# Six weight tiles loaded during the attention: the low parts by ScalarE negation and an accumulating DMA, in place of GpSimd and VectorE subtractions

## The chip, the cores and the metric

The kernel runs on one core of one Trainium2 chip. The metric is the device time of one execution in microseconds, the lower the better. The kernel before took 905.79 us in the median of three runs (904.6 to 907.33).

A core has five engines with instruction queues of their own: PE (TensorE, matrix products), DVE (VectorE), ACT (ScalarE), POOL (GpSimd) and SP (SyncE, which here only issues DMAs). Each works its queue strictly in order, so an instruction that waits holds up all that stand behind it on its engine.

## The reference

One layer of an encoder block over 512 tokens and 16 meta tokens, with 1024 channels. Cut to its main lines:

```python
h = rms_norm(h_res, norm_mix_g[i])
proj = h @ w_in[i]
u, q, k, v, g_ssm, g_attn = jnp.split(proj, split_at, axis=-1)
y_ssm  = ...                 # two-directional state space model on u, GELU, gate
y_attn = gqa_attention(...)  # 16 query heads, 4 key/value heads, softmax over 528 keys
merged = (sigmoid(g_ssm) * (y_ssm @ w_ssm_proj[i])
          + sigmoid(g_attn) * (y_attn @ w_attn_proj[i]))
h_res = h_res + merged @ w_out[i]
h2 = rms_norm(h_res, norm_mlp_g[i])
h_res = h_res + square(relu(h2 @ w_mlp_in[i])) @ w_mlp_out[i]
```

All of it is in float32.

## The kernel before

**Split products.** To get float32 accuracy from the faster matmul type, every operand is split into a high part (a cast to fp32r) and a low part (the operand less its high part). `mm3` issues three matmuls for one product: high by high, high by low and low by high (L159 to L161).

**Loading a weight tile.** `load_w` (L107) makes three tiles of 128 x 1024 values: `wf` by a DMA of 512 KB from SP (L112), `wh` by casts on ACT (L98), and `wl` in one of two ways. The one is a subtraction `wf - wh` on POOL or DVE (L125). The other writes `-wf`, cast to fp32r, into `wl` on ACT (L122) and then lets a DMA issued from POOL add `wf` onto it (L123); what is left in `wl` is the rest that the cast cut off. Which way is taken is `W_ENG[0](i)`: the engine for the low part, or None for the DMA. Each of the three tags has two buffers, so the tiles of load i take the place of those of load i-2, and nothing of a load can be written before the matmuls that read load i-2 are done.

**The attention.** The loop over 16 heads and 4 steps per head issues, for each step: scores of the next head (`sc`, L1102), the maximum on DVE (`mx`, L1106), the exponential on ACT (L1111), the reciprocal of the sum on DVE (`rsm`, L1115), the product on POOL (`ea` or `zT`, L1116), transposes on PE (`atr`, L1126), the split of the transposed block into `ph` on ACT (L98) and `pl` on DVE (L103), and with a lag the matmuls with V (`pv`, L1176). `pvout` copies the result with two ACT copies (`ybuf`, L1146 and L1148).

**Filler.** Between these steps `pump` feeds PE with other work, in the order of `fill_q`: the projections of query groups 2 and 3 (`t_qfull`: two tiles each, matmuls `adp<-wh,hTh` and the like) and five tiles of the attention gate (`t_gate`: one tile each, 24 matmuls `adp<-hTh,wh` and the like). After a query projection its norm and rotation (`norm_rope`) run in small pieces on ACT, DVE and POOL. The casts and low parts of these tiles go through the queue `bgq`, from which `bg_pop` takes three at a time; a scheduler then sets the final order on each engine from priorities and its own model of times.

Nine tiles are loaded for this filler. The first three (query group 2 and the first gate tile) are split with the setting of the stage ahead. The other six, called A to F below, are split with the line

```python
W_ENG[0] = lambda i: (S, WA(V, S, Q)[i % len(WA(V, S, Q))])   # L1166, WA gives (Q, V)
```

so their low parts are made in turn on POOL (A, C, E) and DVE (B, D, F), in two halves of 128 x 512 each. A and B are the two tiles of query group 3, C to F are gate tiles. The same setting serves the tiles after the attention (`w_attn`, `w_out`).

Of the kernel before, what the change touches and what calls it, by code (L numbers as in the profile page):

```python
# [14 lines left out]
ALU = mybir.AluOpType  # L15
# [29 lines left out]
WA = lambda V, S, Q: (Q, V)  # L45
# [25 lines left out]
def hybrid_block(ctx, tc, x, meta, w_in, w_glu, w_ssm, w_attn, w_out, w_m1, w_m2,  # L71
# [3 lines left out]
    V, S, Q, PE = nc.vector, nc.scalar, nc.gpsimd, nc.tensor  # L75
# [16 lines left out]
    W_ENG = [lambda i: (S, Q if i % 2 else V)]  # L92
# [3 lines left out]
    def copy_on(eng, o, i):  # L96
        if eng is S:
            return S.copy(out=o, in_=i)  # L98
        return eng.tensor_copy(out=o, in_=i)
# [8 lines left out]
    def load_w(src, kt, cols):  # L108
        wf = wp.tile([128, kt, cols], F32, tag="wf", bufs=2, name="wf")
        wh = wp.tile([128, kt, cols], F32R, tag="wh", bufs=2, name="wh")  # L110
        wl = wp.tile([128, kt, cols], F32R, tag="wl", bufs=2, name="wl")
        nc.sync.dma_start(out=wf, in_=src.rearrange("(k p) c -> p k c", p=128))  # L112
        i = wcount[0]
        wcount[0] += 1
        eh, el = W_ENG[0](i)
        nh, nl = WS_H[0], 1 if el is None else WS_Q[0] if el is Q else WS_H[0]

        def part(j, n, lo):
            r = slice(kt * j // n, kt * (j + 1) // n)
            if lo and el is None:  # L120

                S.activation(out=wl[:, r], in_=wf[:, r], func=AF.Copy, scale=-1.0)  # L122
                Q.dma_start(out=wl[:, r], in_=wf[:, r], accum_op=ALU.add)  # L123
            elif lo:
                el.tensor_tensor(out=wl[:, r], in0=wf[:, r], in1=wh[:, r].bitcast(F32), op=ALU.subtract)  # L125
            else:
                copy_on(eh, wh[:, r], wf[:, r])
        ops = [(j, nh, False) for j in range(nh)] + [(j, nl, True) for j in range(nl)]
        if bg_on[0]:
            ops = [(j, nh, False) for j in range(nh)] + [(0, 1, True)] if el is None else \  # L130
                [(j, nh, lo) for j in range(nh) for lo in (False, True)]
        for o in ops:
            if bg_on[0]:
                bgq.append((i, lambda o=o: part(*o)))
            else:
                part(*o)
        return wh, wl
# [207 lines left out]
    def t_u(c, res):  # L345
        def run(w):
            wh, wl = w
            H = L // 2
            uT = su1.tile([128, L], F32, tag="uT", bufs=2, name="uT")
            res[c] = uT  # L350
            for hf in range(2):
                ps = dps("ups")[:, :H]
                sl = slice(hf * H, hf * H + H)
                for k in range(KD):
                    mm3(ps, wh[:, k, :], wl[:, k, :], hTh[:, k, sl], hTl[:, k, sl], k == 0, k == KD - 1)
                    yield 0.33
                S.copy(out=uT[:, sl], in_=ps)
        return Task(lambda: load_w(w_in[:, c * 128:c * 128 + 128], KD, 128), run, cost=2 * KD * 0.33)

    def t_gate(m, base, dst, alloc):  # L360
        def run(w):
            ps = alloc()
            for k in range(KD):
                mm3(ps, w[0][:, k, :], w[1][:, k, :], hRh[:, k, :], hRl[:, k, :], k == 0, k == KD - 1)
                yield 0.65
            S.copy(out=dst[:, m, :], in_=ps)
        return Task(lambda: load_w(w_in[:, base + m * 128:base + m * 128 + 128], KD, 128), run, cost=KD * 0.65)

    def load256(base):
        return [load_w(w_in[512 * j:512 * j + 512, base:base + 256], 4, 256) for j in range(2)]  # L370
# [792 lines left out]
    bg_on[0] = True  # L1163
    brk[0] = True
    LBc[0] = LBA
    W_ENG[0] = lambda i: (S, WA(V, S, Q)[i % len(WA(V, S, Q))])  # L1166
    lag = []

    def pv_next():
# [46 lines left out]
    h_st.close()  # L1216


    WS_H[0], WS_Q[0] = 1, 1
    h2_st = ExitStack()  # L1220
    h2p = h2_st.enter_context(tc.tile_pool(name="h2p", bufs=1, side="right", reuse_waits="tile"))
# [34 lines left out]
    for m in range(KD):  # L1256
        wh, wl = load_w(w_attn[:, m * 128:m * 128 + 128], KD, 128)
# [323 lines left out]
```

## Time and profile before

| | before |
|---|---|
| median of three runs | 905.79 us |
| profiled execution, its time | 902.95 us |
| profiled execution, its span | 901.0 us |
| PE busy | 844.8 us, 94% |
| DVE busy | 676.2 us, 75% |
| ACT busy | 521.9 us, 58% |
| POOL busy | 193.2 us, 21% |

The span runs from the first to the last instruction on the chip; 1.95 us lie around it. PE is the busiest engine over the whole. The attention loop runs from about 282 to 467 us. Busy shares over the span say little of one stage, so the attention is read from windows, from waits and from the instructions in order of time.

### The profile page before, as it was taken

What the parts mean: (1) busy time and instruction counts of PE and PEld (TensorE: products, weight loads), DVE (VectorE), ACT (ScalarE), POOL (GpSimd) and SP (SyncE); (2) the same over time, 40 slices, a digit from 0 to 9 for tenths busy, and PEclk for the clock granted to TensorE, in tenths of its full rate; (3) what the DMA queues carried; (4) which work ended last, traced back from release to release, by engine and by line L of the source; (5) the groups of instructions that cost most, each with busy time, mean ns of one, the idle gap of its engine ahead of it and who ended that gap; (6) DMA issues with size and microseconds to landing.
All of it is one profiled execution on the core that took longest, in us unless ns stands there. A gap on an engine that the chain in (4) does not pass through costs nothing.

```text
span 901.0 us, 13081 instructions
## 1 busy us (share of the span) xinstructions
PE 844.8 (94%) x4798; PEld 721.6 (80%) x4798; DVE 676.2 (75%) x1217; ACT 521.9 (58%) x916; POOL 193.2 (21%) x185
## 2 busy tenths in 40 slices
PE   6989999978998989799989999999999999999994
PEld 4988888767886979688878888888888888888884
DVE  6997799779898697867775536747767577776687
ACT  5446776547745557578784245656555655555543
POOL 1001100001021567566534450010100010000000
PEclk9999999999999999999999999999999999999998
DMA  7245533212122020011024343466656556575302
GB/s 240 68 98 113 130 83 78 76 48 70 56 87 71 29 70 5 21 46 49 20 77 134 111 142 119 149 163 164 161 143 164 147 157 168 136 187 134 100 1 93
DMA packets 97473, 92.52 MB, mean 103 GB/s; under 512 B 4465, under 2 KB 79793, under 8 KB 97410
## 3 DMA queue, kind: packets, MB, share of 16 engines
q1 hardware_dynamic: 87824, 69.25, 25.3%
q0 software_dynamic: 5168, 18.40, 10.6%
q10 hardware_dynamic: 4418, 4.04, 1.6%
q8 instruction: 38, 0.62, 0.3%
q14 instruction: 25, 0.20, 0.1%
HBM read 69.03 MB, written 2.10 MB: 79 GB/s over the span
## 4 chain that ended last, share of the span: by engine, by line
PE 74%; DVE 14%; ACT 6%; DMA 3%; issue 3%; POOL 1%; DVEq 0%; ACTq 0%; POOLq 0%; SPq 0%
PE m L161 6%; PE m L160 6%; PE m L159 6%; PE o L161 5%; PE o L159 5%; PE o L160 5%; PE pv L1176 3%; PE sc L1102 2%; PE atr L1126 2%; DVE wl L125 2%; PE gps L159 2%; PE gps L161 2%; PE gps L160 2%; PE adp L159 2%; PE adp L160 2%
## 5 line engine op out<-in xcount | busy, mean ns | idle before, releaser
L98 ACT CAST wh<-wf 128x512 fp32r<-128x512 f32 (+1 forms) x120 | 90.0, 778 | 99.8 <-PE m L160 60.7
L1447 DVE TENSOR_TENSOR ybuf<-o,ybuf 128x1024 f32<-128x1024 f32 x52 | 63.6, 1222 | 67.9 <-PE o L161 67.8
L123 POOL DMA_DIRECT2D wl<-wf x35 | 30.3, 865 | 377.4 <-ACT wl L122 299.5
L161 PE MATMUL m<-h2h,wl 128*128 128x512 f32 (+1 forms) x272 | 102.4, 377 | 0.8 <-DVE wl L125 0.8
L160 PE MATMUL m<-h2l,wh 128*128 128x512 f32 (+1 forms) x272 | 102.5, 377 | 0.2 <-DVE h2l L103 0.2
L159 PE MATMUL m<-h2h,wh 128*128 128x512 f32 (+1 forms) x272 | 102.3, 377 | 0.3 <-ACT h2h L98 0.2
L160 PE MATMUL o<-ol,fh 128*128 128x512 f32 (+1 forms) x216 | 83.2, 385 | 0.0
L159 PE MATMUL o<-oh,fh 128*128 128x512 f32 (+1 forms) x216 | 83.2, 385 | 0.0
L161 PE MATMUL o<-oh,fl 128*128 128x512 f32 (+1 forms) x216 | 83.2, 385 | 0.0
L125 DVE TENSOR_TENSOR wl<-wf,wh 128x512 fp32r<-128x512 f32 (+1 forms) x65 | 57.3, 900 | 13.4 <-ACT wh L98 13.2
L161 PEld LDWEIGHTS m<-h2h,wl 128*128 128x128 f32 x272 | 51.2, 188 | 10.5 <-DVE wl L125 1.3
L159 PEld LDWEIGHTS m<-h2h,wh 128*128 128x128 f32 x272 | 51.1, 188 | 10.1 <-ACT h2h L98 0.5
L160 PEld LDWEIGHTS m<-h2l,wh 128*128 128x128 f32 x272 | 51.2, 188 | 9.8 <-DVE h2l L103 0.4
L1106 DVE TENSOR_REDUCE mx<-sc 128x1 f32<-128x528 f32 x64 | 44.8, 702 | 12.7 <-PE sc L1102 11.9
L103 DVE TENSOR_TENSOR pl<-atr,ph 128x512 fp32r<-128x512 f32 x64 | 43.5, 684 | 9.3 <-ACT ph L98 8.5
L98 ACT CAST ph<-atr 128x512 fp32r<-128x512 f32 x64 | 37.1, 584 | 18.1 <-PE atr L1126 17.6
L161 PEld LDWEIGHTS o<-oh,fl 128*128 128x128 f32 x216 | 40.6, 188 | 8.1
L160 PEld LDWEIGHTS o<-ol,fh 128*128 128x128 f32 x216 | 40.6, 188 | 8.1
L159 PEld LDWEIGHTS o<-oh,fh 128*128 128x128 f32 x216 | 40.6, 188 | 8.0
L1116 POOL TENSOR_TENSOR ea<-zT,rsm 128x528 f32<-128x528 f32 x32 | 34.2, 1069 | 21.2 <-DVE rsm L1115 20.3
L122 ACT ACTIVATE wl<-wf 128x1024 fp32r<-128x1024 f32 x35 | 36.8, 1050 | 0.9 <-PE kvps L160 0.9
L1176 PE MATMUL pv<-ph,Vhl 128*128 128x256 f32 x128 | 34.6, 294 | 2.2 <-ACT ybuf L1148 1.4
(403 smaller groups left out, 2477.9 us busy)
## 6 DMA issues: line engine op xcount, KB each, us to landing
wl<-wf POOLq DMA_DIRECT2D x35, 512.0 KB, 4.4
wf<-in_w_in_dram SPq DMA_DIRECT2D x32, 512.0 KB, 4.0
wf<-in_w_m_dram SPq DMA_DIRECT2D x32, 512.0 KB, 4.1
q<-in_w_m_dram SPq DMA_DIRECT2D x32, 512.0 KB, 4.5
ybuf<-in_x_dram SPq DMA_DIRECT2D x8, 512.0 KB, 4.0
wf<-in_w_attn_dram SPq DMA_DIRECT2D x8, 512.0 KB, 4.0
wf<-in_w_out_dram SPq DMA_DIRECT2D x8, 512.0 KB, 3.2
wf<-in_w_ssm_dram SPq DMA_DIRECT2D x4, 512.0 KB, 3.5
```

The source lines that it names most:

```text
L98: return S.copy(out=o, in_=i)
L103: b = el.tensor_tensor(out=l, in0=src, in1=h.bitcast(F32), op=ALU.subtract)
L122: S.activation(out=wl[:, r], in_=wf[:, r], func=AF.Copy, scale=-1.0)
L123: Q.dma_start(out=wl[:, r], in_=wf[:, r], accum_op=ALU.add)
L125: el.tensor_tensor(out=wl[:, r], in0=wf[:, r], in1=wh[:, r].bitcast(F32), op=ALU.subtract)
L159: PE.matmul(out=o, lhsT=lh, rhs=rh, start=first, stop=False, skip_group_check=goes_on)
L160: PE.matmul(out=o, lhsT=lh, rhs=rl, start=False, stop=False, skip_group_check=goes_on)
L161: return PE.matmul(out=o, lhsT=ll, rhs=rh, start=False, stop=last, skip_group_check=goes_on)
L1106: g0 = V.tensor_reduce(out=mx, in_=sc[:, :, :NL], axis=AX.XY, op=ALU.max, negate=True)
L1116: pend.append(lambda: Q.tensor_tensor(out=en, in0=e, in1=rs_.to_broadcast([128, L]), op=ALU.mult))
L1176: PE.matmul(out=pvt[0][:, 256 * f:256 * f + 256], lhsT=vw, rhs=pw, start=left == [8, 9], stop=left == [0, 0])
L1447: V.tensor_tensor(out=x2q[r][h], in0=z, in1=x2q[r][h], op=ALU.add)
```

## The change

In the attention `W_ENG` gives None for the low part, so tiles A to F are made by ACT's negated copies and an accumulating DMA from POOL. The copies are made in two halves, the DMA once for the whole tile, and in the queue both casts now come ahead of both negations. Behind the attention the setting of before is put back, so `w_attn` and `w_out` are split as they were.

```diff
                 S.activation(out=wl[:, r], in_=wf[:, r], func=AF.Copy, scale=-1.0)
-                Q.dma_start(out=wl[:, r], in_=wf[:, r], accum_op=ALU.add)
+                if j == n - 1:
+                    Q.dma_start(out=wl, in_=wf, accum_op=ALU.add)
...
         if bg_on[0]:
-            ops = [(j, nh, False) for j in range(nh)] + [(0, 1, True)] if el is None else \
+            ops = [(j, nh, lo) for lo in (False, True) for j in range(nh)] if el is None else \
                 [(j, nh, lo) for j in range(nh) for lo in (False, True)]
...
-    W_ENG[0] = lambda i: (S, WA(V, S, Q)[i % len(WA(V, S, Q))])
+    W_ENG[0] = lambda i: (S, None)
...
     h_st.close()
+    W_ENG[0] = lambda i: (S, WA(V, S, Q)[i % len(WA(V, S, Q))])
     WS_H[0], WS_Q[0] = 1, 1
```

The new lines move the numbers: L123 becomes L124, lines below it go up by one, and those behind L1219 by two. Six DVE and six POOL subtractions leave, twelve ACT negations and six DMAs come in. SP's order is the same.

The scheduler also moves other instructions. On PE, around tile E (`adp<-hTh,wh` and its fellows are the gate matmuls, `sc`, `atr` and `pv` belong to the attention), before:

```order
L159 MATMUL adp<-hTh,wh 128x512
L160 MATMUL adp<-hTl,wh 128x512
L1102 MATMUL sc<-Kh,qst 128x264 x2
L1102 MATMUL sc<-Kl,qst 128x264 x2
L161 MATMUL adp<-hTh,wl 128x512
L159 MATMUL adp<-hTh,wh 128x512
L160 MATMUL adp<-hTl,wh 128x512
```

And in the changed kernel, 11 rows behind the same two matmuls with `wh`:

```order
L1177 MATMUL pv<-pl,Vhl 128x256
L1103 MATMUL sc<-Kh,qst 128x264 x2
L1103 MATMUL sc<-Kl,qst 128x264 x2
L1127 MATMUL atr<-ident,zT 128x128
L1127 MATMUL atr<-ident,ea_3210 128x128
L1127 MATMUL atr<-ident,zT 128x128
L1127 MATMUL atr<-ident,ea_3210 128x128
L162 MATMUL adp<-hTh,wl 128x512
L160 MATMUL adp<-hTh,wh 128x512
L161 MATMUL adp<-hTl,wh 128x512
```

The first gate matmul that reads E's `wl` now stands behind 20 attention matmuls more, and all 22 that are left of the tile stand there in one run. Before, 17 of the 22 were spread among those 20, and the last five stood at the same place.

On ACT, around the split of tile E (`gbuf` is the copy of tile D's result, `qst` a split of the queries), before:

```order
L1111 ACTIVATE zT,sm<-sc,mx 128x528
L98 CAST wh<-wf 128x512 x2
L990 CAST qst<-atr 64x512
L1111 ACTIVATE rt,sm<-sc,mx 128x528
L98 CAST ph<-atr 128x512
L990 CAST qst<-atr 64x512
```

And in the changed kernel:

```order
L1112 ACTIVATE zT,sm<-sc,mx 128x528
L98 CAST wh<-wf 128x512
L122 ACTIVATE wl<-wf 128x512
L98 CAST wh<-wf 128x512
L367 COPY gbuf<-adp 128x512
L991 CAST qst<-atr 64x512
L1112 ACTIVATE rt,sm<-sc,mx 128x528
L122 ACTIVATE wl<-wf 128x512
L98 CAST ph<-atr 128x512
```

One negation has moved in ahead of the exponential, the other behind it, ahead of the `ph` cast.

On POOL at the same place, before:

```order
L1116 TENSOR_TENSOR ea_3210<-zT,rsm 128x528
L125 TENSOR_TENSOR wl<-wf,wh 128x512 x2
L1116 TENSOR_TENSOR ea_3210<-rt,rsm 128x528
L1149 TENSOR_TENSOR ybuf<-ybuf 64x512
L125 TENSOR_TENSOR wl<-wf,wh 128x1024
```

And in the changed kernel:

```order
L1117 TENSOR_TENSOR ea_3210<-rt,rsm 128x528
L124 DMA wl<-wf 128x1024
L1117 TENSOR_TENSOR ea_3210<-zT,rsm 128x528
L1150 TENSOR_TENSOR ybuf<-ybuf 64x512
L124 DMA wl<-wf 128x1024
L126 TENSOR_TENSOR wl<-wf,wh 128x1024
```

E's DMA stands behind the product that stood behind E's subtractions, and F's DMA has come in ahead of the subtraction of the first `w_attn` tile.

Elsewhere in the attention, the gate matmuls of tile D (10 of 24) and most of the first pass of query group 3 move back by some 15 to 23 rows on PE; those of tiles C and F keep their places. On ACT both negations of B stand ahead of a `ph` cast, and those of C ahead of its own casts and of an exponential.

## Rows read from the trace of the kernel before

**Rows 1.** The page: span; busy us, share and instructions of PE.

```profile
span 901.0 us, 13081 instructions
PE 844.8 (94%) x4798; PEld 721.6 (80%) x4798; DVE 676.2 (75%) x1217; ACT 521.9 (58%) x916; POOL 193.2 (21%) x185
```

**Rows 2.** Windows: length, busy of PE, PEld, DVE, ACT, POOL; granted clock; DMA.

```profile
350.00:370.00 20.00, 16.27 (x124) 15.13 (x124) 16.19 (x35) 11.47 (x25) 13.21 (x12) 0.97 0.09 28
390.00:410.00 20.00, 20.00 (x133) 17.45 (x132) 14.27 (x28) 17.48 (x37) 14.06 (x13) 1.00 0.14 38
410.00:430.00 20.00, 17.85 (x135) 15.54 (x134) 15.33 (x30) 16.10 (x37) 15.24 (x13) 1.00 0.15 43
```

**Rows 3.** PE's waits, 275 to 465 us: us in total, times, longest.

```profile
PE atr L1126 <- DVE pl L103: 4.9, 6, 2.6
PE pv L1176 <- DVE pm L1140: 3.2, 4, 1.1
```

**Rows 4.** Low parts before, groups of 265:462 (busy, mean ns), then by time.

```profile
L125 POOL TENSOR_TENSOR wl<-wf,wh 128x512 fp32r<-128x512 f32 x6 | 7.6, 1294 | 0.0
...
331.84 2.61 DVE L125 TENSOR_TENSOR wl<-wf,wh 128x512 fp32r<-128x512 f32 x2
380.21 1.42 DVE L125 TENSOR_TENSOR wl<-wf,wh 128x512 fp32r<-128x512 f32 x1 [0.35 <-ACT wh L98]
```

**Rows 5.** ACT half tile, group of 265:462; L123: ns min/median/max; its landing.

```profile
L98 ACT CAST wh<-wf 128x512 fp32r<-128x512 f32 x22 | 12.6, 618 | 0.8 <-PE adp L161 0.7
...
L123 POOL DMA_DIRECT2D wl<-wf x35: 852/862/918, 55.8 to 842.9; - x35
...
DMA to landing us min/median/max: 4.4/4.4/6.2
```

**Rows 6.** By time, near tile A: start us, us; the wait in brackets.

```profile
319.94 1.22 DVE L171 TENSOR_SCALAR rst<-st 128x16 int32<-128x16 int32 x1
325.13 0.18 DVE L177 TENSOR_TENSOR rst<-rsy 128x16 f32<-128x16 f32 x1
327.07 0.52 PE L1102 MATMUL sc<-Kh,qst 128*128 128x264 f32 x2 [1.47 <-ACT zT L1111]
```

**Rows 7.** By time, near tile B.

```profile
330.92 0.59 ACT L98 CAST ph<-atr 128x512 fp32r<-128x512 f32 x1
331.57 0.38 PE L1176 MATMUL pv<-ph,Vhl 128*128 128x256 f32 x1 [0.68 <-ACT ph L98]
```

**Rows 8.** By time, near tile C.

```profile
355.17 1.14 ACT L98 CAST wh<-wf 128x512 fp32r<-128x512 f32 x2 [0.74 <-PE adp L161]
356.22 0.70 ACT L1111 ACTIVATE rt<-sc,mx 128x528 f32<-128x528 f32 x1
367.16 0.33 PE L1126 MATMUL atr<-ident,zT 128*128 128x128 f32 x1 [2.62 <-DVE pl L103]
```

**Rows 9.** By time, near tile D.

```profile
383.11 0.39 PE L1176 MATMUL pv<-ph,Vhl 128*128 128x256 f32 x1 [0.92 <-ACT ybuf L1148]
```

**Rows 10.** By time, tile E and what follows its last matmul.

```profile
399.87 0.70 ACT L1111 ACTIVATE rt<-sc,mx 128x528 f32<-128x528 f32 x1
402.30 1.08 POOL L1116 TENSOR_TENSOR ea<-rt,rsm 128x528 f32<-128x528 f32 x1
401.41 0.40 PE L161 MATMUL adp<-hTh,wl 128*128 128x512 f32 x1
401.64 0.40 PE L159 MATMUL adp<-hTh,wh 128*128 128x512 f32 x1
408.56 0.40 PE L161 MATMUL adp<-hTh,wl 128*128 128x512 f32 x1
408.76 1.05 ACT L98 CAST wh<-wf 128x1024 fp32r<-128x1024 f32 x1 [0.37 <-PE adp L160]
```

**Rows 11.** Windows over two idle stretches of PE and what followed; columns as above.

```profile
291.70:294.00 2.30, 0.00 (x0) 0.00 (x0) 2.30 (x3) 0.88 (x3) 2.30 (x3) 0.97 0.00 0
294.00:297.50 3.50, 3.49 (x17) 3.50 (x18) 1.41 (x4) 1.91 (x4) 2.63 (x3) 0.53 0.29 76
```

## The prediction

> **What bounds the kernel now.** I read the page's head first: 901.0 us of span, PE busy for 844.8 of them [rows 1]. The profiled execution took 902.95 us, so 1.95 us lie around the span; the median of the runs shown is 905.79 us, 2.84 us above it. Sums are made on the 902.95 and then moved by 2.84.
>
> Only the attention is edited, so next come windows of it. PE is busy for 16.27 of 20 us in one window, for all 20 in another and for 17.85 in a third [rows 2]. So PE sets the pace over long stretches and is stopped in short ones. PE's waits say by whom: most for DVE, 4.9 us for `pl` and 3.2 us for `pm` [rows 3]. An edit here pays only where it shortens one of these stops, and costs wherever it makes a new one, because PE works in order. Last I read the instructions in order of time around each of the six tiles, and compare when `wl` is ready with when PE asks for it.
>
> **The change, priced by kind.** Out go six POOL halves of 1.29 us, 7.6 us [rows 4], and six DVE halves; the two of B took 2.61 us together, one of D 1.42 us [rows 4], and 0.7 us each for the remaining three makes some 6 us. In come twelve ACT negations. The trace has no negation of a half tile, but a cast of the same shape takes 0.62 us [rows 5], or 0.57 in a row of two [rows 8], so 12 x 0.6 = 7 us on ACT. In come six DMA issues of 0.86 us on POOL, 5 us, and what matters more, each lands 4.4 us after its issue at the median, 6.2 at most [rows 5]. A subtraction of 1.3 us made `wl` ready; now the last negation, POOL's turn and 4.4 us stand in that place.
>
> The Trainium skill, page "DMA: Bandwidth & Descriptors", section "Anatomy of one DMA — SWDGE (gpsimd) path", gives about 2.0 us fixed and 436 KB per us, which for 512 KB is an estimate of 3.2 us. The 35 DMAs of this very kind in the trace say 4.4 [rows 5], and the measurement decides; by the page the forecast below would be 1.2 us lower.
>
> **The change, tile by tile.**
>
> A: POOL's two subtractions leave just where the small DVE steps of the query norm run. There such a step took 1.22 us, and 0.18 us a little later [rows 6]. Four of them were so long, and PE waited 1.47 us for the exponential behind them [rows 6]. POOL's rotation products move up and lengthen some of them again. I take one step's worth, -1.2 us; ends 0 and -2.5 (two steps and a half). A's `wl` is first read behind B's casts, which come after the gate tile between them is done, so its DMA costs nothing.
>
> B: both negations stand ahead of a `ph` cast for which PE already waited 0.68 us [rows 7]. They delay it by 1.14 us; some of it may be won back by DVE's 2.61 us. +0.9 us. PE's matmuls with B's `wl` were moved back, and by 4.4 us of landing they are met within about a microsecond; ends +0.3 and +2.2.
>
> C: the negations stand ahead of the casts at 355.17 and so push the exponential at 356.22 by 1.14 us [rows 8]. From there ACT's queue runs without a pause to the norm's square, DVE's small steps and the `pl` for which PE waited 2.62 us at 367.16 [rows 8]. +1.1 us; ends 0 (if DVE, not ACT, sets that stop) and +1.6 (if the DMA lands after PE's call too).
>
> D: one negation comes ahead of the `ph` cast and of the two `ybuf` copies, for the second of which PE waited 0.92 us [rows 9]. +0.6 us; ends 0 and +1.2. The matmuls were moved back by enough for the DMA.
>
> E is the largest. One negation pushes the exponential of 399.87 to about 400.4, the second follows it and ends near 401.9. The DMA stands behind POOL's product of 1.08 us [rows 10], which may now start at about 402.0. So issue is near 403.1 and landing near 407.5. PE ran E's `wl` matmuls from 401.41 to 408.56, 0.23 us apart [rows 10]. With 22 of them now in one run behind the attention's matmuls, PE can be there at 408.56 - 21 x 0.23 = 403.7, or, as an estimate, near 405 if two more negations of 0.57 us on ACT hold up the exponentials. It stands until 407.5 and starts the last of the 22 at 407.5 + 21 x 0.23 = 412.3, against 408.56: +3.7 us. Behind it on ACT stands the cast of the next `w_attn` tile, which waits for E's last matmul already now, 0.37 us [rows 10]; all `ph` casts queue behind that cast, so the attention itself is late by as much. Ends: 0, if the DMA lands by 404, and +5.4, with the clock (below).
>
> F: its matmuls come after a long stretch of attention work that hides the landing; 0, ends -0.6 and +0.6, a half negation either way. The source tiles are held until the DMA has landed instead of until the subtraction, so the loads behind them start later; a whole tile's matmuls lie between such a load and its use and hide that. If that cover were gone it would be 4.4 us a tile.
>
> Given back: behind E PE idles for 2.15 us between 410 and 430 [rows 2]. Part of that is waiting for DVE, which now catches up: -1.5 us; ends 0 and -2.2.
>
> Sum: -1.2 + 0.9 + 1.1 + 0.6 + 3.7 + 0 - 1.5 = **+3.6 us**, so 906.6 us for an execution like the profiled one and 905.79 + 3.6 = 909.4 us at the median. All low ends together are -5.0, all high ends +11.
>
> **The rivals.**
>
> *Faster, by relief of DVE and POOL.* PE waits on DVE for 4.9 + 3.2 us [rows 3], and small DVE steps are seven times longer beside POOL work [rows 6]. If `wl` lands before PE calls and the freed 6 us of DVE and 7.6 us of POOL come off the stops, half of those 8.1 us goes: 905.79 - 4.0 = 901.8. It decides at E: landing by about 404. Against it: the DVE steps that PE waits for mostly lie in A and C, and in C POOL's subtractions were over before them. The Trainium skill, page "GPSIMD Engine Reference", section "8. Key points", says that GpSimd and VectorE share SBUF interfaces and contend; by that rule DVE should gain, and the trace agrees for A.
>
> *Hidden.* From 390 to 410 PE is busy all the time [rows 2]; if PE has work in its queue for each delay and A's gain pays for B and C, the time is 905.8 within 2.7.
>
> *Slower still, by the clock.* After 2.30 us with no PE work the granted clock was 0.53 for 3.5 us [rows 11], half of full speed, the lower of the two levels; 3.5 x 0.47 = 1.6 us were lost. A stop of 2.5 us at E would do this again, and one at C makes a stop longer that is 2.62 us already: 909.4 + 1.6 to 909.4 + 3.3, so 911 to 912.7.
>
> That the change doesn't do what it says is left out: the order shows all six DMAs in place.
>
> **How the numbers follow.** The forecast, 909.4, has 0.38 (its own range 906.5 to 911); the clock on top of it 0.14; hidden 0.27; relief 0.21. A measurement of this kernel can tell about 0.3%, 2.7 us, from no change. Relief mostly falls beyond that, 0.18 of it, hidden wholly within, and of the forecast 0.03 falls within too. So faster 0.18, same 0.27 + 0.03 + 0.03 = 0.33, slower 0.35 + 0.14 = 0.49. To leave out no more than 2 in 10, the range goes from 902 (within relief) to 914.
>
> **What would show it.** Right: PE waiting for DMA `wl` at a gate matmul for 2 us or more near 405 us, the last matmul of E about 4 us later against the start of the attention, and ACT's first `w_attn` cast late by the same. The stop near 367 us longer by about 1 us. DVE's small steps near 320 us shorter. SP's waits no worse. Wrong: no wait of PE for `wl` at all, or an attention that ends earlier than before; then the landing or PE's arrival at E is mis-sized, or DVE was the bound all along.

## The result, and the profile after

The changed kernel took 914.68 us in the median of four executions (912.27 to 915.41), beside 905.19 us for the kernel before: a ratio of 1.0098, 95% interval 1.0082 to 1.0114. So it is slower, by 9.5 us where 3.6 were forecast, and the time lies just outside the range of 902 to 914. A second set of six executions, with a median of 914.55 us beside 905.55, gave the same ratio, 1.0098 (1.0067 to 1.0130).

The profiled execution took 912.27 us, 910.1 of them the span. The page's head, to be held against [rows 1]:

```profile
span 910.1 us, 13094 instructions
...
PE 850.9 (93%) x4798; PEld 725.2 (80%) x4798; DVE 669.2 (74%) x1211; ACT 528.4 (58%) x928; POOL 189.3 (21%) x185
```

ACT has 6.5 us more, DVE 7.0 and POOL 3.9 us less, much as priced. PE does the same 4798 matmuls and is busy 6.1 us longer: a busy PE that does no more work is a slower PE. Part of this is the pair of executions: the mean granted clock was 0.985 here and 0.991 in the profile before, where the kernel before has 0.987 on average. All of the difference arises in the attention or ahead of it. Both kernels compute 64 exponentials in the loop, in the same sequence, so each can be paired with its like. The one at the loop's start is 1.4 us later than before, although the instructions up to there are the same; that is spread between executions, not an effect of the change. The one behind tile E (423.82, before 414.72) is 9.1 us later, and so are all that follow, to the end. So 7.7 us of this pair arise in the attention.

Windows of the attention (length, busy of PE, PEld, DVE, ACT, POOL; granted clock; DMA):

```profile
330.00:350.00 20.00, 17.45 (x125) 16.25 (x126) 11.92 (x25) 13.62 (x32) 10.53 (x11) 0.91 0.33 80
360.00:390.00 30.00, 24.21 (x145) 20.41 (x142) 20.75 (x43) 18.64 (x40) 16.60 (x16) 0.89 0.15 36
390.00:410.00 20.00, 19.07 (x124) 16.05 (x123) 13.56 (x27) 15.71 (x36) 11.34 (x11) 1.00 0.25 57
410.00:430.00 20.00, 16.60 (x109) 14.04 (x108) 10.32 (x21) 13.84 (x29) 11.31 (x10) 1.00 0.52 129
```

The granted clock, 0.91 and 0.89 in the first two, was 1.00 and 0.94 over the same times before:

```profile
330.00:350.00 20.00, 17.47 (x139) 16.37 (x138) 16.42 (x29) 13.62 (x31) 11.90 (x11) 1.00 0.09 27
360.00:390.00 30.00, 25.14 (x154) 21.69 (x153) 24.04 (x46) 16.51 (x36) 15.84 (x15) 0.94 0.12 35
```

So 0.09 x 20 = 1.8 and 0.05 x 30 = 1.5 us more of work were lost there to the lower level of the clock. A slow stretch near 333 us is not new in itself: the versions with C, D or E alone, which are as the kernel before up to 350 us, have one too (0.88 over 326 to 340 us). There the next stops were shorter by as much, and the exponentials behind them were no later. In the changed kernel they lose 2.4 us between 326 and 343 us; in the version with small DMAs, whose clock is full from 330 to 350 us, 0.4 us.

In the last two windows the clock is full, and PE is busy 0.9 and 1.25 us less than before [rows 2]. PE's waits over the attention name what is new (us in total, times, longest; beside [rows 3]):

```profile
PE atr L1127 <- DVE pl L103: 5.6, 7, 1.8
PE pv L1177 <- DVE pm L1141: 3.9, 4, 1.9
PE adp L162 <- DMA wl<-wf: 2.5, 2, 2.1
...
PE pv L1177 <- ACT ph L98: 1.8, 3, 1.0
```

Third stands the wait for the accumulating DMA, which the kernel before did not have in the attention. By time, around tile E:

```profile
403.50 0.63 ACT L122 ACTIVATE wl<-wf 128x512 fp32r<-128x512 f32 x1
405.50 0.71 ACT L1112 ACTIVATE rt<-sc,mx 128x528 f32<-128x528 f32 x1
406.19 0.63 ACT L122 ACTIVATE wl<-wf 128x512 fp32r<-128x512 f32 x1
407.27 1.07 POOL L1117 TENSOR_TENSOR ea<-rt,rsm 128x528 f32<-128x528 f32 x1 [2.48 <-DVE rsm L1116]
408.27 0.86 POOL L124 DMA_DIRECT2D wl<-wf  x1
412.74 0.50 PE L162 MATMUL adp<-hTh,wl 128*128 128x512 f32 x1 [2.09 <-DMA wl<-wf]
417.66 0.40 PE L162 MATMUL adp<-hTh,wl 128*128 128x512 f32 x1
417.86 1.05 ACT L98 CAST wh<-wf 128x1024 fp32r<-128x1024 f32 x1 [3.41 <-PE adp L161]
```

This is the chain that the prediction drew: the second negation behind the exponential, POOL's product, the DMA, PE standing until it lands 4.4 us later, 22 matmuls in one run, and ACT's next cast held up behind them.

### The profile page after: what moved, and what is told of

Same layout as the page of the kernel before. It is cut to its first block, busy times and chain, and to the rows that moved or that the text cites. A ratio compares the mean times of both kernels' runs of the same rounds, so it can differ in the third digit from the quotient of the medians.

```text
span 910.1 us, 13094 instructions
## 1 busy us (share of the span) xinstructions
PE 850.9 (93%) x4798; PEld 725.2 (80%) x4798; DVE 669.2 (74%) x1211; ACT 528.4 (58%) x928; POOL 189.3 (21%) x185
## 4 chain that ended last, share of the span: by engine, by line
PE 73%; DVE 13%; ACT 6%; DMA 4%; issue 3%; POOL 1%; DVEq 0%; ACTq 0%; POOLq 0%; SPq 0%
PE m L162 6%; PE m L161 6%; PE m L160 6%; PE o L160 5%; PE o L162 5%; PE o L161 5%; PE pv L1177 3%; DMA wl<-wf 3%; PE sc L1103 2%; PE adp L162 2%; PE adp L160 2%; PE adp L161 2%; PE gps L160 2%; PE atr L1127 2%; PE gps L162 2%
## 5 line engine op out<-in xcount | busy, mean ns | idle before, releaser
L124 POOL DMA_DIRECT2D wl<-wf x41 | 35.3, 862 | 379.5 <-ACT wl L122 271.5
L126 DVE TENSOR_TENSOR wl<-wf,wh 128x512 fp32r<-128x512 f32 (+1 forms) x59 | 51.4, 890 | 12.4 <-ACT wh L98 12.3
L103 DVE TENSOR_TENSOR pl<-atr,ph 128x512 fp32r<-128x512 f32 x64 | 43.6, 685 | 15.2 <-ACT ph L98 14.6
L122 ACT ACTIVATE wl<-wf 128x1024 fp32r<-128x1024 f32 (+1 forms) x47 | 44.2, 944 | 1.5 <-PE kvps L161 0.9
L1127 PE MATMUL atr<-ident,ea 128*128 128x128 f32 x192 | 36.4, 284 | 2.4 <-DVE pl L103 2.3
```

Of the source, the lines that this page charges most:

```text
L103: b = el.tensor_tensor(out=l, in0=src, in1=h.bitcast(F32), op=ALU.subtract)
L124: Q.dma_start(out=wl, in_=wf, accum_op=ALU.add)
L1127: PE.transpose(ps[:, j * 256 + q * 128:j * 256 + q * 128 + 128], ea[2 * f + q][:, c:c + 128], ident)
```

## The experiments

The change is taken apart at the line that chooses the engine. It becomes a list, one entry for each of the tiles A to F; `None` is the new way, Q and V are the subtractions of the kernel before. For tile A alone:

```diff
-    W_ENG[0] = lambda i: (S, None)
+    wa0 = wcount[0]
+    W_ENG[0] = lambda i: (S, (None, V, Q, V, Q, V)[i - wa0])
```

Two numbers are given for each kernel. One is the ratio to the kernel before on the same chip. The other is the work lost to the low level of the clock, averaged over the executions: span times one less the mean granted clock. It is an estimate of what the clock cost, since a stop that follows a slow stretch gets a little shorter. Over 89 executions the kernel before lost 12.1 us (standard error 0.3) and over 10 the changed one 15.2 (0.8). The column "clock" is the difference to the kernel before that ran beside it; "rest" is the difference of the mean times less that.

| kernel | median, us | ratio (95%) | clock, us | rest, us |
|---|---|---|---|---|
| A alone | 904.98 | 0.9997 (0.9981 to 1.0014) | +2.3 | -1.9 |
| B alone | 907.20 | 1.0031 (1.0014 to 1.0048) | +1.9 | +0.7 |
| C alone | 908.68 | 1.0036 (1.0021 to 1.0052) | +0.7 | +2.3 |
| D alone | 906.66 | 1.0003 (0.9986 to 1.0020) | +1.1 | -0.1 |
| E alone | 909.24 | 1.0048 (1.0032 to 1.0063) | -0.5 | +4.6 |
| all but E | 908.99 | 1.0040 (1.0024 to 1.0055) | +2.1 | +1.5 |
| changed kernel again | 914.55 | 1.0098 (1.0067 to 1.0130) | +2.0 | +7.2 |
| negations on DVE | 910.90 | 1.0065 (1.0042 to 1.0089) | +1.5 | +4.9 |
| POOL adds, no DMA | 906.96 | 1.0010 (0.9996 to 1.0024) | +0.9 | +0.2 |
| small DMA | 909.24 | 1.0030 (1.0014 to 1.0047) | +1.2 | +1.8 |
| E ahead | 913.30 | 1.0093 (1.0072 to 1.0115) | +3.6 | +4.8 |
| A new, E ahead | 906.90 | 1.0021 (1.0007 to 1.0035) | +2.0 | -0.2 |

The kernel before, run beside each, had medians of 904.89 (A, B, E, negations on DVE), 905.66 (C, D, POOL adds, small DMA), 905.55 (the changed kernel again, E ahead, A new with E ahead) and 905.21 us (all but E). The clock column carries an error of 0.7 to 1.5 us, so a single entry of it says little and the common sign says more.

**Tile A alone** (the edit above).

> Only tile A takes the negation and the accumulating DMA; B to F are split as before. Theory 1 (the freed POOL time shortens the small VectorE steps of the query norm, nothing waits for A's DMA): 1.5 us faster than before (ratio 0.998), PE's wait of 1.47 us near 327 us gone. Rival 1 (PE hides it, or ScalarE's two negations eat it): ratio 1.000 within 0.001.

The time did not move, but both of its parts did. At A the paired exponentials come 1.5 us earlier. The 1.47 us wait near 327 us is gone, and one of 1.20 us for a `pl` stands 4 us later. The DVE chain from the first small step to the next maximum takes 4.5 us instead of 6.1: three steps of 1.07 to 1.21 us in place of four of 1.07 to 1.32. All seven run beside a POOL instruction and end within 0.06 us of its end, so what leaves with the subtractions comes back in part with POOL's rotation products, as the prediction said. Then the stop near 367 us is followed by a longer stretch of low clock than in the kernel before. Ten us around it, first this kernel, then the kernel before:

```profile
364.00:374.00 10.00, 6.27 (x27) 4.97 (x26) 9.37 (x19) 5.02 (x12) 7.41 (x7) 0.70 0.00 0
```
```profile
364.00:374.00 10.00, 6.27 (x30) 4.91 (x29) 9.37 (x19) 5.07 (x12) 7.28 (x7) 0.83 0.00 0
```

PE stands still for the same 3.7 us in both, but the granted clock over the window is 0.70 against 0.83, which is 1.3 us. On the means, the gain in stops of 1.9 us went back to the clock. Why the clock should lose more here is not shown: the instructions near 367 us are those of the kernel before, and of the other versions of which that is true B alone has the longer stretch too, D alone and E alone the shorter one.

**Tile B alone.**

```diff
+    W_ENG[0] = lambda i: (S, (Q, None, Q, V, Q, V)[i - wa0])
```

> Only tile B is changed. Theory 1 (B's two negations ahead of a ph cast lengthen a stop of PE near 332 us by 0.4 us, and a clock drop of 3.4 us at half speed follows): about 2 us slower than before (ratio 1.0023), granted clock near 0.5 somewhere in 333 to 337 us. Rival 2 (only the landing of a DMA costs, and PE does not wait for B's): ratio 1.000 within 0.001, clock 1.00 there.

The stop is where the prediction put it, and of its size:

```profile
334.74 0.39 PE L1178 MATMUL pv<-ph,Vhl 128*128 128x256 f32 x1 [1.72 <-ACT ph L98]
```

1.72 us against 0.68 in the kernel before [rows 7] is 1.04 us; 0.6 us of it are left at the later exponentials. The expected fall of the clock at 333 us did not come (328 to 340 us at 1.00), but the slow stretch behind the stop at 367 us was longer: 0.89 over 360 to 390 us, before 0.94.

**Tile E alone.**

```diff
+    W_ENG[0] = lambda i: (S, (Q, V, Q, V, None, V)[i - wa0])
```

> Only tile E is changed. Theory 1 (PE stands for E's landing, 22 gate matmuls run late, and the next w_attn cast on ScalarE holds all ph casts behind it): 3.7 to 4 us slower than before (ratio 1.0042), PE waits for the DMA into wl for 2 us or more. Rival 3 (the loss is two negations on a full ScalarE): 1.2 us (ratio 1.0013), no such wait.

```profile
406.89 0.50 PE L162 MATMUL adp<-hTh,wl 128*128 128x512 f32 x1 [2.37 <-DMA wl<-wf]
```

The exponentials behind E are 4.0 us later against those ahead of it. The granted clock over 400 to 420 us is 1.00. E is the largest single cost, and it comes with the landing in front of PE, without the clock.

**The negations on DVE instead of ACT**, six DMAs kept:

```diff
+            elif lo and el == "D":
+                V.tensor_scalar(out=wl[:, r], in0=wf[:, r], scalar1=-1.0, scalar2=None, op0=ALU.mult)
+                if j == n - 1:
+                    Q.dma_start(out=wl, in_=wf, accum_op=ALU.add)
```

> All six tiles by accumulating DMA, but the negated copies are made on VectorE, so ScalarE has nothing added. Theory 1 (landing and negations both cost): the waits for the landing at E stay, the stops that ScalarE's negations lengthened near B and C go back, so 3 to 5 us slower than before (ratio 1.003 to 1.0055). Rival 2 (landing alone): all of the 9 us stays (ratio 1.010). Rival 3 (ScalarE's load alone): ratio 1.000 within 0.001.

Without ACT's 7.4 us of negations two thirds of the loss stay, somewhat more than the theory's 1.0055 though within the interval. PE still waits 2.0 us for DMAs, and the exponentials fall back 3.1 us at E. ACT's load alone is not the cause. How much of the loss it is does not follow from this version, since its negations make stops of their own on DVE (2.38 us for an exponential at 335 us, 3.07 us for a `pm` at 373 us).

**ACT's negations kept, POOL adds instead of the DMA.**

```diff
+            elif lo and el == "P":
+                S.activation(out=wl[:, r], in_=wf[:, r], func=AF.Copy, scale=-1.0)
+                Q.tensor_tensor(out=wl[:, r], in0=wl[:, r].bitcast(F32), in1=wf[:, r], op=ALU.add)
```

> All six tiles keep ACT's negated copies in the order of casts first, but POOL adds the tile onto them in two halves instead of a DMA: the landing of 4.4 us is gone, the twelve negations on ACT stay, and POOL keeps its 7.6 us. Theory: E's cost falls from 4.2 us to some 0.5 to 1.5 us and no wait of PE for a DMA is left; the stops by negations at B, C and D stay, with one or two stretches of low clock more, so 904.9 + 2.5 to + 5.5, a ratio of 1.003 to 1.006. Rival, landing alone: 1.000. Rival, ACT's load alone: 1.010 as in the changed kernel.

1.0010, below the theory's range; the rival, landing alone with 1.000, lies within the interval. With the landing gone, the twelve negations on ACT, six halves fewer on DVE and six more on POOL cost 1.1 us of mean time in sum. The stop at B stays (1.71 us for `ph`), and E costs 0.8 us. The order of some 90 matmuls differs too, so the landing is the main difference to the changed kernel, but not the only one. Over 390 to 430 us PE is back to nearly what [rows 2] show (20.00 and 17.85):

```profile
390.00:410.00 20.00, 19.88 (x126) 16.93 (x125) 12.40 (x25) 17.41 (x38) 14.49 (x13) 1.00 0.14 41
410.00:430.00 20.00, 18.24 (x137) 16.01 (x136) 14.27 (x28) 16.42 (x36) 14.96 (x13) 1.00 0.19 55
```

**The same kernel with small DMAs.**

```diff
+            elif lo and el == "S":
+                S.activation(out=wl[:, r], in_=wf[:, r], func=AF.Copy, scale=-1.0)
+                if j == n - 1:
+                    Q.dma_start(out=wl[:, 0:1, 0:16], in_=wf[:, 0:1, 0:16], accum_op=ALU.add)
```

> As the changed kernel, but each of the six DMAs adds only 16 of the 1024 columns (the addition of the others is left out). It tells the fixed part of a landing from the part that goes with the 512 KB. Theory: the landing is near 2 to 3 us instead of 4.4, so E's stop falls from 2.1 us to about 0 to 0.7 and E's cost by 1.4 to 2.4 us, the rest stays as in the changed kernel: a ratio of 1.007 to 1.0085. Rival, the six transfers themselves and not their latency disturb the loads or SBUF: most of the 9.5 us goes, 1.000 to 1.003. Rival, ACT's load alone: 1.010.

The DMA's own line in the attention, issue and landing:

```profile
L128 POOL DMA_DIRECT2D wl<-wf x6: 860/866/889, 322.0 to 409.8; - x6
...
DMA to landing us min/median/max: 2.0/2.0/2.1
```

The landing falls from 4.4 to 2.0 us, PE's waits for DMAs from 2.5 to 0.4 us, and E's delay from 4.0 to 2.1 us, as the theory had it. But two thirds of the loss came back, 1.0030 where the theory had 1.007 to 1.0085, which is the edge of the first rival's range. In the profiles the exponentials fall back 2.3 us over the attention instead of 7.7. Of the 5.4 us between, 1.9 are at E. The slow stretch behind B is missing here and the one near 371 us is half as long, together 3.4 us less work lost, and PE does not wait for D's DMA. So the rest came back mostly at the clock, which on the means loses 1.2 us more than before (error 0.9) where the changed kernel loses 3.1. Whether the transfers themselves have a part in that is not told apart. Apart from some 90 of the 4798 matmuls the order on PE is that of the changed kernel. So of 4.4 us of landing 2.0 are fixed and 2.4 go with the 512 KB. The Trainium skill, page "DMA: Bandwidth & Descriptors", section "Anatomy of one DMA — SWDGE (gpsimd) path", gives about 2.0 us for the fixed part, and the trace agrees; for the variable part it would say 1.2 us at 436 KB per us, and the runs show twice that for this accumulating form.

**Tile C alone and tile D alone.**

```diff
+    W_ENG[0] = lambda i: (S, (Q, V, None, V, Q, V)[i - wa0])
```

> Only tile C (the first gate tile of the loop) is split the new way, the other five as before. Theory (stops by negations ahead of an exponential, plus what the clock then loses): the stop near 367 us is longer by about 1.1 us and the clock drops there for two stretches instead of one, 1.7 us more, so 904.9 + 1.1 to 904.9 + 2.8, a ratio of 1.001 to 1.003. Rival (only landings cost, and C's matmuls come late enough): 1.000, with no change at 367 us.

C cost more than its term, 1.0036. Around 367 us PE waits 0.49, 1.80 and 1.92 us in place of 2.62 and 1.10, half a microsecond more. Of 2.5 us by which the exponentials fall back in all, some 1.9 came 35 us later, where tile E stands and is split as before: there PE now waits 0.87 us for a `pl` that DVE makes behind two maxima, and 1.10 us for another at 414 us.

```profile
402.81 0.63 PE L986 MATMUL atr<-ident,kvraw 128*128 128x128 f32 x4 [0.87 <-DVE pl L103]
```

```diff
+    W_ENG[0] = lambda i: (S, (Q, V, Q, None, Q, V)[i - wa0])
```

> Only tile D is split the new way. Prediction's term: the negation ahead of the split of the transposed block delays PE by 0.6 us, a ratio of 1.0007, and the stop at 367 us, which lies ahead of D, is as before. Rival (landing alone decides): D's matmuls with the low part were moved back far enough, 1.000. The two differ by less than the timing tells, so it is the trace that decides: exponentials behind 383 us later by 0.6 us, or not later at all.

D alone is within what the timing tells, 1.0003. In the trace waits of 0.20 and 0.92 us [rows 9] have become four of 0.71, 0.54, 0.28 and 0.31 us, 0.7 us more, close to the prediction's term of 0.6; the exponentials behind them are 1.1 us later against those ahead. D's DMA landed after 4.4 us and PE did not wait for it. The profile also has a stretch of low clock at 330 us, ahead of D, where its instructions are those of the kernel before and that one's profile had none. Where the clock falls differs between executions of the same instructions, which is why single profiles are not enough for it.

**The changed kernel once more.**

> The changed kernel once more, beside the two below on one chip, for its mean granted clock over more executions and for a second profile. Theory (part of the loss is the clock): the work lost to a low clock, span times one less the mean granted clock, is about 3 us above that of the kernel before (15.3 us in four executions against 11.8), and the rest of the difference, some 6 us, is PE standing still; the ratio 1.009 to 1.011. Rival (the low stretches come by chance in the profiled execution and cost nothing on average): the same work is lost to the clock in both kernels, within 0.7 us.

Its profile shows the stops over 0.5 us at the same places and of nearly the same lengths, and two things that came out otherwise. D's DMA landed after 6.3 us instead of 5.1 and PE waited 1.59 us for it instead of 0.39, and the stop at E was followed by a slow stretch (414 to 419 us at 0.68):

```profile
PE adp L162 <- DMA wl<-wf: 3.7, 2, 2.1
```
```profile
414.00:419.00 5.00, 3.93 (x11) 3.07 (x12) 1.36 (x3) 2.75 (x6) 2.17 (x2) 0.68 0.61 156
```

The clock loses 2.0 us more than in the kernel before beside it (errors 1.3 and 0.7); with the first four executions, and against all 89 of the kernel before, it is 3.1 us (0.9). The rival of pure chance, within 0.7 us, is unlikely but not shut out.

**Tile E ahead.** E gets a source and a low part of its own and is loaded and negated with D:

```diff
+        if i + 1 in due:
+            xf, xl = early[i + 1] = [kp.tile([128, KD, 128], d, name=n) for d, n in ((F32, "xf"), (F32R, "xl"))]
+            nc.sync.dma_start(out=xf, in_=due[i + 1].rearrange("(k p) c -> p k c", p=128))
...
+                S.activation(out=xl[:, r], in_=xf[:, r], func=AF.Copy, scale=-1.0)
+                if j:
+                    Q.dma_start(out=xl, in_=xf, accum_op=ALU.add)
```

> The changed kernel, but tile E gets its source and its low part in two buffers of their own and is loaded and negated with tile D, one tile ahead, so its accumulating DMA is issued before D's and some 15 us before PE asks. Negations, their number and the six DMAs stay; only E's landing is hidden. Theory: no wait of PE for the DMA of E is left and 3 to 4.5 us come back, 910 to 912 us, a ratio of 1.0045 to 1.007. Rival (what E costs is ACT's negations in front of the exponentials): 1.008 to 1.010, as they only move to D.

No wait for E's DMA is left, and yet 1.0093. The two negations now stand in front of D's `ph` cast, and PE waits there instead:

```profile
387.21 1.16 ACT L149 ACTIVATE xl<-xf 128x512 fp32r<-128x512 f32 x2
390.04 0.39 PE L1194 MATMUL pv<-ph,Vhl 128*128 128x256 f32 x1 [1.58 <-ACT ph L98]
```

1.58 us against 0.54 in the changed kernel. D's DMA, now second in the queue behind E's, landed after 7.7 us and PE waited 0.9 us for it. The rest fell from 7.2 to 4.8 us, but the clock took 1.7 us more than in the changed kernel beside it, with an error of 1.5, so the time did not fall measurably. The rival was nearer than the theory: what is pulled ahead on ACT must have its own gap there.

**A new and E ahead, the others as before.**

```diff
+    W_ENG[0] = lambda i: (S, (None, V, Q, V, None, V)[i - wa0])
```

> The kernel before, but A is split the new way and E the new way with its own buffers, one tile ahead; B, C, D and F are subtracted as before. It keeps the one gain that the traces showed (A, 1.5 us) and hides E's landing. Theory: PE stands still 1.5 to 2 us less than in the kernel before; if the clock loses no more than there, 903 us and a ratio of 0.998; if it loses 2.3 us more, as with A alone, 1.000 to 1.001. Rival (E's ACT work alone costs 1 us or more): 1.001 to 1.003.

The one version built to beat both kernels did not: 1.0021, in the rival's range. Its PE stands still no more than before (rest -0.2), and the clock loses 2.0 us more. At 385 us PE waits 1.44 us for a `pl`, where it waited 0.9 us before.

**All but E.**

```diff
+    W_ENG[0] = lambda i: (S, (None, None, None, None, Q, None)[i - wa0])
```

> The changed kernel with tile E alone put back to POOL's two subtractions; A to D and F stay on negations and DMAs. Theory (the tiles' costs add up): the changed kernel less the 4.0 to 4.3 us that E alone cost, 910.3 to 910.7 us, a ratio of 1.0055 to 1.006, with no wait of PE for the DMA of E and the work lost to a low clock still 2 to 3 us above the kernel before. Rival (later stops swallow what E costs, so that taking E away only uncovers them): 1.008 to 1.010. Rival (E is all of it, the other tiles cancel): 1.000 to 1.003.

1.0040: taking E out of the changed kernel gives back 0.58%, some 5.3 us, more than the 4.3 it cost alone. Neither swallowed (1.008 and up) nor all of it (1.003 and below) holds. The other tiles together cost 3.6 us, less than the sum of A, B, C and D alone (-0.3 + 2.8 + 3.3 + 0.3 = 6.1 us by their ratios). That difference is about twice its error; one reason could be that B and C share the slow stretches around 333 and 370 us, which is not shown. In this profile too PE waited 1.9 us for D's DMA, which took 6.6 us to land.

## Why the prediction was wrong in size, step by step

**Direction and place held.** The largest cost is E, by the landing in front of PE; in the versions that take the landing away (POOL adds) or halve it (small DMA), nine tenths and two thirds of the loss are gone. The chain of E was right in each link. By E everything is 5.1 us late; less that, the issue was at 403.2 (forecast 403.1), the landing at 407.6 (407.5), PE's call at 405.6 (403.7 to 405), the last matmul at 412.6 (412.3). The term of 3.7 us measured 4.0 in the trace and 4.3 in the time of E alone.

**What failed first: the 1.5 us given back behind E.** They are 0. The paired exponentials are 9.1 us late right behind E and 9.1 at the attention's end. DVE is less busy from 410 to 430 us, 10.32 us against 15.33 [rows 2], but PE's waits for it are as long as before, first here, then before:

```profile
421.07 0.30 PE L1127 MATMUL atr<-ident,zT 128*128 128x128 f32 x1 [0.58 <-DVE pl L103]
424.35 0.50 PE L1177 MATMUL pv<-pm,Vm 64*128 64x256 f32 x2 [0.59 <-DVE pm L1141]
```
```profile
411.96 0.30 PE L1126 MATMUL atr<-ident,zT 128*128 128x128 f32 x1 [0.58 <-DVE pl L103]
415.24 0.50 PE L1176 MATMUL pv<-pm,Vm 64*128 64x256 f32 x2 [0.53 <-DVE pm L1140]
```

So they are the way from a transpose over ACT and DVE back to PE rather than a queue on DVE that a pause could empty.

**What failed second: the clock was kept out of the forecast.** It stood as a rival with 0.14, at one or two stretches on top, 1.6 to 3.3 us. Measured, the changed kernel loses 3.1 us (0.9) more to it (in the attention its two profiles spend 13.7 and 17.1 us at the lower level, the profile before 6.8), and all the kernels here but E alone, which lost 0.5 us less, lost 0.7 to 3.6 us more. D alone is among them with 1.1, though its edit lies behind the stop at 367 us, so about as much is the spread of the measurement. The prediction looked only at lone stops of over 2 us, as in [rows 11]. The trace shows the low level also after two shorter ones in a row:

```profile
369.10 0.33 PE L1127 MATMUL atr<-ident,zT 128*128 128x128 f32 x1 [1.79 <-DVE pl L103]
...
371.68 0.79 PE L1177 MATMUL pv<-pm,Vm 64*128 64x256 f32 x2 [1.92 <-DVE pm L1141]
...
374.19 0.63 PE L160 MATMUL adp<-hTh,wh 128*128 128x512 f32 x1
```

From there a gate matmul takes 0.43 us instead of 0.23 to the next. That this is the mechanism is argued from rows of this kind; the slow stretches lie near 333 us (B) and 372 us in both profiles of the changed kernel, and behind E, where the rival put one, in one of the two. That the change costs clock time on average is shown only as well as the errors allow.

**Terms of the middle tiles.** A's -1.2 was right in the trace (-1.5) and nothing in the time, where the clock lost as much more. The prediction's relief rival leaned on DVE sharing SBUF interfaces with POOL. The Trainium skill, page "GPSIMD Engine Reference", section "8. Key points", names as the case of contention DVE instructions in a 2-port perf mode or with two SBUF inputs. The seven slow steps at A agree that POOL holds DVE up (in which mode they ran the profile does not tell); of PE's stops only A's is seen to get shorter by it. B's +0.9 was right as a stop (1.04) and a third of the time (+2.8). C's +1.1 measured about +3 in the time and 2.5 in the trace, 1.9 of it at tile E's place, behind other DVE work; that was no step of the prediction. D's +0.6 is 0.7 in PE's waits, but "moved back by enough for the DMA" failed: in the changed kernel PE waited 0.39 and 1.59 us for D's DMA, since that landed after 5.1 and 6.3 us instead of 4.4 (why, in the last section). F's 0 was not tried alone, but holds in the trace: from the exponential behind E on nothing is added.

**The sum put right.** 3.6 us, without the give-back +1.5, with the clock +3.1, E's 0.3 to 0.6 more, and D's DMA 0.4 to 1.6: 8.9 to 10.4 us, beside 9.0 and 9.5 in the two sets. It is not a proof: C's second part and whatever makes the tiles together cheaper than one by one are left out, with opposite signs, and are not told apart.

**The rivals.** Relief is refuted as a whole and right for A; hidden is refuted. Slower by the clock (911 to 912.7) had the right mechanism and size; its base was too low by the give-back, by E's 0.3 to 0.6 and by D's DMA.

## What to carry to other kernels

A subtraction replaced by an accumulating DMA trades engine time (here two halves of 1.3 us) for latency (a landing of 4.4 us), so it pays only where the tile is made well ahead of its reader; count from the last negation, through the issuing engine's queue, to the landing, and look where the reader then stands. Waits that are a round trip over other engines did not shrink here when those got idle, so do not book a give-back unless a backlog is visible. A DMA that lands just in time is not safe: leave room for a landing 1 to 2 us late. Where TensorE is near its bound, price a pair of stops of 1 to 2 us for the clock too, and judge that by the mean granted clock of many executions, not by one profile.

## What the runs showed of the hardware that was not expected

Where the clock falls is not a property of the instructions alone: over 89 executions of the kernel before the mean granted clock ranged from 0.980 to 0.993 and the time from 902 to 911 us. One stretch at the lower level loses some 1.7 us (0.14 x 12 over 364 to 376 us in the kernel before). A stop of 2.09 us at E was followed by the low level in one profile of the changed kernel and not in the other.

The same accumulating DMA of 512 KB landed after 4.4 us for tiles A to C and E (to within 0.3 us), but for tile D after 4.4 us alone and 5.1, 6.3 and 6.6 us in three kernels where the tiles ahead were also new, with no load by SP beside it. The packets tell more. Each such DMA sends sixteen completions. Fifteen of D's came within 4.4 us of the issue in all three, as in D alone; the last came 0.76, 1.94 and 2.25 us behind them. One packet of the queue that loads instructions, 16 KB, ran at that time. In the second profile of the changed kernel:

```profile
q0 software_dynamic: 144, 0.52, 40.9%
q8 instruction: 1, 0.02, 0.9%
wl<-wf POOLq DMA_DIRECT2D x1, 512.0 KB, 6.3
```

It ran from 394.51 to 395.44 us, and the last 4 KB of D's data from 395.43 on; in D alone the like packet came 0.1 us behind the landing. Over all fourteen profiles, 358 such DMAs had no other load beside them. Of the 40 that overlapped an instruction load, 24 sent their last completion over 0.5 us late; of the other 318 none did, and none took over 4.7 us. So the late landings go with loads of instructions. That the two shared a DMA engine, and that the load so held up the landing, is inferred from the times; the profile does not name the engine.
